# A convolution stage laid out anew: weight lows on GpSimd, pairs of channel groups summed as one, more native fp32 products

## The chip, the core and the metric

The kernel runs on one core of a Trainium2 chip. Its engines are TensorE (PE, with its weight loads as PEld), VectorE (DVE), ScalarE (ACT), GpSimd (POOL) and SyncE (SP), which issues the DMA transfers. Each engine works through its own list of instructions in order; an instruction starts when the semaphores that it waits on are there. The metric is the device time of one execution in microseconds.

## The reference

One inference step of a two-layer decoder trunk over 256 prompt tokens and 8 sample tokens, which share the weights. Layer 0 has a Conformer convolution as its mixer, layer 1 an mLSTM; each is followed by a layer norm, a gated feed-forward block with a three-tap convolution, another norm, and a gated per-layer embedding. The change lies in the mixer of layer 0:

```python
def conformer_conv(x, past, w_in, b_in, w_dw, b_dw, ln_g, ln_b, w_out, b_out):
    a, gt = jnp.split(x @ w_in + b_in, 2, axis=-1)      # 2048 -> 2 x 2048
    u = a * jax.nn.sigmoid(gt)
    y, new_past = causal_dwconv(u, past, w_dw, b_dw)    # 31 taps per channel
    y = jax.nn.silu(layer_norm(y, ln_g, ln_b))
    return y @ w_out + b_out, new_past
...
x = layer_norm(ALPHA * x + mix, ln_mix_g[i], ln_mix_b[i])
```

## The kernel before

Everything is kept feature by feature: a tile holds 128 channels (one group) by 264 tokens, and 2048 channels are 16 groups. A matrix product runs over 16 pieces of 128 input channels (k). Weights come from memory in fp32, three raw buffers of four k pieces by 512 columns. Most are split into a high part `whi` (a cast on ACT to fp32r) and a low part `wlo` (raw minus high, on DVE or POOL), and a product is three fp32r matmuls: high weight with the high and the low part of X (`XH`, `XL`), low weight with `XH`. A native product takes the raw weight and fp32 `X` in one instruction, which the trace shows as two records, and needs neither high nor low part.

The mixer goes through the 16 channel groups in blocks (`BLOCKS`), seven of two groups and two of one. `conv_mixer` calls `wblock` for a block's gate and value columns (L216 the load, L226 native products, L234 the cast, L235 the low, L250 to L259 the matmuls). `NAT` says which pairs of k pieces are native, `PLO` which lows POOL makes; DVE makes the others. Then the block's gates: a sigmoid on ACT (L546), which frees the gate's accumulator, the product `U` = value times gate in PSUM on DVE (L141), and its copy to SBUF (`us4`, L555).

The 31 taps of a group are shared out. Two go to ACT alone (L557, L559). `GT` taps are a product on ACT (L564) and a sum on POOL (L138, `cscr`). `PT` taps, in the last blocks, are matmuls with a diagonal weight matrix (L588); POOL makes the diagonals in the first block (L504). The others are one scalar-tensor-tensor on DVE each, from `U` into `Y` (L141). A join on DVE (L138, `Y<-Y,cscr`) adds POOL's sums to `Y`. The sample tokens need the past state times the taps (`xs`, `SCM`).

Behind the last block comes the layer norm: `ln_pre` sums the first 12 groups, shifts them by their mean and sums their squares, `ln` adds the last four groups and normalises. Then the output projection starts, in which `WOL` names the lows of the first block that POOL makes. `residual` scales X by ALPHA for the sum behind it.

A scheduler sets each engine's order ahead of time by priorities (`tc.high_priority`): casts and lows may be made up to five steps ahead of their matmuls (five `hlp` buffers). DMA issues all stand in SP's list.

Of the kernel before, what the change touches and what calls it, by code (L numbers as in the profile page):

```python
# [108 lines left out]
def _body(ctx, tc, nc, I, O):  # L109
# [94 lines left out]
    def wblock(W, cols, rhs, nk, acc, k0=0, loe=None, hook=None, fine=False, native=None, hold=(), lag=0, stage=0, side=None):  # L204
# [3 lines left out]
        for kg in range(0, nk, 4):  # L208
            kn = min(4, nk - kg)
            raw = rawp.tile([P, 4, 512], F32, name="raw")  # L210
            for ka, step in ([(0, 2), (2, 2)] if fine else [(0, kn)]):
# [8 lines left out]
            for h0 in range(0, kn, 2):  # L220
                for f in (side or {}).get(kg + h0, ()):
                    f()
                if native and native(kg + h0):
                    for kc in (kg + h0, kg + h0 + 1):
# [6 lines left out]
                r = raw[:, h0:h0 + 2, :width]  # L231
# [12 lines left out]
                for k2 in range(2):  # L244
# [32 lines left out]
    def ln_pre(Y, pm=None):  # L277
        a = t4("lna")
        tt(a, Y[:, 0:4], Y[:, 4:8], ALU.add)
        tt(a, a, Y[:, 8:12], ALU.add)  # L280
# [198 lines left out]
    def conv_mixer():  # L479
# [15 lines left out]
        def diags():  # L495
# [20 lines left out]
        late = []  # L516
        for bi, (c0, n) in enumerate(blocks):
            last = bi == len(blocks) - 1
            acc = accs(2 * n)
            wblock(W, [(D + c0 * P, n * P), (c0 * P, n * P)], x_rhs, NC, acc,  # L520
                   loe=lambda k, bi=bi: g if _pick(PLO[bi], k // 2) else v,
                   native=lambda k, bi=bi: _pick(NAT[bi], k // 2) or (bi == 0 and k // 2 in N0), hook=load if bi == 0 else None, fine=bi == 0)
            if bi == DGB:
                diags()
            if last:
# [5 lines left out]
                emb = embed(embed_load(0, pl), None, [us4[:, 4:8], us4[:, 0:4]])  # L531
                with tc.high_priority(PREP):
                    shift, sd, sq = ln_pre(Y, accs(1)[0])
            for q in SCM.get(bi, ()):
# [4 lines left out]
                tt(xs, xs, w.unsqueeze(2).to_broadcast([P, 4, NB, 30]), ALU.mult)  # L539
                ys = Y[:, 4 * q:4 * q + 4, SEQ:]  # L540
                v.tensor_reduce(ys, xs, AX.X, ALU.add)
                tt(ys, ys, pc("cv_b_dw", 4 * q, 4).unsqueeze(2).to_broadcast([P, 4, NB]), ALU.add)
# [4 lines left out]
            Z = []
            gt = GT[bi]
            for j in range(n):
                ch, a = c0 + j, acc[n + j]  # L550
# [8 lines left out]
                act(z[:, 1:SEQ], w[:, 0:SEQ - 1], AF.Copy, scale=pc("cv_w_dw", ch * CW + 29))  # L559
                Z.append(z)  # L560
            for t in range(28, 28 - gt, -1):
                for j in range(n):
                    z2 = slot(4, 8)
                    act(z2[:, 30 - t:SEQ], us4[:, (2 * bi + j) % 8, 0:226 + t], AF.Copy, scale=pc("cv_w_dw", (c0 + j) * CW + t))  # L564
                    tt(Z[j][:, 30 - t:SEQ], Z[j][:, 30 - t:SEQ], z2[:, 30 - t:SEQ], ALU.add, e=g)
            if (c0 + n) % 4 == 0:

                q = c0 + n - 4
                w = pc("cv_w_dw", q * CW, 4 * CW).rearrange("p (c t) -> p c t", t=CW)[:, :, 30:31]
                uw = smp.tile([P, 4, NB], F32, name="uw")  # L570
                tt(uw, us[:, q:q + 4], w.to_broadcast([P, 4, NB]), ALU.mult)
                tt(Y[:, q:q + 4, SEQ:], Y[:, q:q + 4, SEQ:], uw, ALU.add)
            pt = PT.get(bi, 0)
# [5 lines left out]
            def join(n=n, c0=c0, Z=Z):  # L579
# [525 lines left out]
```

## Time and profile before

| | us |
|---|---|
| median of 3 runs | 2574.08 (2572.9 to 2576.8) |
| the profiled execution | 2575.43 |
| its span | 2573.7 |
| PE busy | 2514.4 (98%) |
| DVE busy | 1656.2 (64%) |
| ACT busy | 1284.8 (50%) |
| POOL busy | 318.2 (12%) |

The shares are means over stages that differ: POOL has nearly all its work in the first tenth of the span, which is the convolution stage. Times in the rows below count from the start of the span.

### The profile page before, as it was taken

To read this page: it belongs to the slowest core of one execution; us is meant where nothing else is said; L and a number is where in the kernel's file an instruction comes from. 1 tells how busy PE (TensorE), PEld (TensorE's weight loads), DVE (VectorE), ACT (ScalarE), POOL (GpSimd) and SP (SyncE) were. 2 spreads that over 40 slices of the span, in tenths; PEclk is the share of its full clock that TensorE was granted. 3 is DMA by queue.
4 is the path that set the end of the run, shared out by engine and by line. 5 is a ranking of instruction groups with operands and counts; after the bars stand their busy time and mean duration, and the time that the engine had idled before them with its cause. 6 is when DMAs were issued, how large, how long until landed. Compare 5 with 4: busy or idle time off the path is not lost.

```text
span 2573.7 us, 47727 instructions
## 1 busy us (share of the span) xinstructions
PE 2514.4 (98%) x20130; PEld 2489.2 (97%) x20130; DVE 1656.2 (64%) x2382; ACT 1284.8 (50%) x1801; POOL 318.2 (12%) x320
## 2 busy tenths in 40 slices
PE   8898999999999999999999999999999999999999
PEld 8897999999999999999999998999999999999999
DVE  6999786555444555478667777685555445555595
ACT  5676555444334444356557665464444334444363
POOL 7898120000000000011000000020000000000020
PEclk9999999999999999999999999999999999999999
DMA  7546445655555556555677777555565556556553
GB/s 248 178 133 195 159 159 183 195 180 181 180 181 181 180 167 222 179 171 181 211 236 237 248 257 238 198 173 181 169 192 182 181 174 187 180 179 205 176 173 133
DMA packets 266696, 486.56 MB, mean 189 GB/s; under 512 B 12362, under 2 KB 68426, under 8 KB 265938
## 3 DMA queue, kind: packets, MB, share of 16 engines
q1 hardware_dynamic: 266482, 483.52, 58.2%
q8 instruction: 157, 2.57, 0.4%
q14 instruction: 57, 0.47, 0.1%
HBM read 465.77 MB, written 19.68 MB: 189 GB/s over the span
## 4 chain that ended last, share of the span: by engine, by line
PE 86%; DVE 5%; DMA 3%; POOL 3%; issue 2%; ACT 1%; SPq 0%; POOLq 0%; DVEq 0%; ACTq 0%
PE acc L253 27%; PE acc L250 27%; PE acc L252 24%; PE acc L259 3%; POOL cscr L138 1%; DMA out_cT<-X 1%; DVE wlo L235 1%; POOL wlo L235 1%; DVE Y L138 1%; PE acc L452 1%; DVE Y L141 1%; DMA X<-in_cT 1%; DMA spare<-scr 1%; PE acc L226 1%; POOL u L504 0%
## 5 line engine op out<-in xcount | busy, mean ns | idle before, releaser
L235 DVE TENSOR_TENSOR wlo<-raw,whi 128x1024 fp32r<-128x1024 f32 (+1 forms) x770 | 960.0, 1252 | 801.7 <-ACT whi L234 751.0
L234 ACT CAST whi<-raw 128x1024 fp32r<-128x1024 f32 x812 | 846.0, 1045 | 999.7 <-PE acc L252 952.6
L253 PE MATMUL acc<-XH,wlo 128*128 128x264 f32 x4264 | 1190.7, 286 | 17.4 <-DVE wlo L235 9.3
L250 PE MATMUL acc<-XH,whi 128*128 128x264 f32 x4264 | 1193.0, 286 | 6.6 <-ACT cscr L546 5.0
L252 PE MATMUL acc<-XL,whi 128*128 128x264 f32 x3696 | 1049.0, 285 | 0.0
L253 PEld LDWEIGHTS acc<-XH,wlo 128*128 128x128 f32 x4264 | 803.1, 189 | 20.5 <-DVE wlo L235 10.3
L250 PEld LDWEIGHTS acc<-XH,whi 128*128 128x128 f32 x4264 | 801.0, 189 | 9.9 <-ACT cscr L546 5.4
L252 PEld LDWEIGHTS acc<-XL,whi 128*128 128x128 f32 x3696 | 700.8, 190 | 0.2
L235 POOL TENSOR_TENSOR wlo<-raw,whi 128x1024 fp32r<-128x1024 f32 (+1 forms) x42 | 97.6, 2327 | 1696.1 <-DVE X L138 1506.0
L253 PE MATMUL acc<-ha,wlo 128*128 128x264 f32 x1024 | 290.0, 285 | 0.0
L250 PE MATMUL acc<-ha,whi 128*128 128x264 f32 x1024 | 288.4, 285 | 0.0
L252 PE MATMUL acc<-ha,whi 128*128 128x264 f32 x960 | 271.9, 284 | 0.0
L250 PE MATMUL acc<-xo,whi 128*128 128x264 f32 x768 | 221.4, 289 | 2.2 <-ACT vv L877 1.5
L253 PE MATMUL acc<-xo,wlo 128*128 128x264 f32 x768 | 218.9, 287 | 0.0
L252 PE MATMUL acc<-xo,whi 128*128 128x264 f32 x720 | 207.7, 289 | 0.0
L253 PEld LDWEIGHTS acc<-ha,wlo 128*128 128x128 f32 x1024 | 193.1, 189 | 0.0
L250 PEld LDWEIGHTS acc<-ha,whi 128*128 128x128 f32 x1024 | 191.9, 188 | 0.1
L252 PEld LDWEIGHTS acc<-ha,whi 128*128 128x128 f32 x960 | 181.3, 189 | 0.1
L250 PEld LDWEIGHTS acc<-xo,whi 128*128 128x128 f32 x768 | 144.6, 188 | 3.3 <-ACT vv L877 1.7
L253 PEld LDWEIGHTS acc<-xo,wlo 128*128 128x128 f32 x768 | 144.7, 189 | 0.6
L252 PEld LDWEIGHTS acc<-xo,whi 128*128 128x128 f32 x720 | 135.9, 189 | 0.6
L138 POOL TENSOR_TENSOR cscr<-cscr 128x254 f32<-128x254 f32 (+10 forms) x140 | 123.8, 909 | 11.6 <-ACT cscr L564 10.4
(283 smaller groups left out, 2495.4 us busy)
## 6 DMA issues: line engine op xcount, KB each, us to landing
raw<-in_ff_w_gate SPq DMA_DIRECT2D x88, 1024.0 KB, 5.1
raw<-in_ff_w_up SPq DMA_DIRECT2D x88, 1024.0 KB, 5.1
raw<-in_ff_w_down SPq DMA_DIRECT2D x88, 1024.0 KB, 5.0
raw<-in_pl_w_gate SPq DMA_DIRECT2D x32, 1024.0 KB, 5.1
raw<-in_ml_w_in SPq DMA_DIRECT2D x32, 1024.0 KB, 5.9
raw<-in_cv_w_in SPq DMA_DIRECT2D x48, 512.0 KB, 4.8
raw<-in_cv_w_out SPq DMA_DIRECT2D x16, 1024.0 KB, 5.1
raw<-in_ml_w_in SPq DMA_DIRECT2D x32, 512.0 KB, 5.1
```

The lines of the kernel that those rows point to most:

```text
L138: return e.tensor_tensor(o, a, b, op)
L141: return v.scalar_tensor_tensor(o, a, sc, b, op0, op1)
L226: pe.matmul(acc[j], raw[:, kc - kg, j * P:(j + 1) * P], X[:, kc], start=kc == 0, stop=kc == nk - 1)
L234: whi = s.copy(hi[:, :, :width], r)
L235: wlo = e.tensor_tensor(lo[:, :, :width], r, f32(hi[:, :, :width]), ALU.subtract)
L250: pe.matmul(acc[j], wh, xh, start=kc == 0, stop=False)
L252: pe.matmul(acc[j], wh, xl, start=False, stop=False)
L253: wlast[0] = pe.matmul(acc[j], wl, xh, start=False, stop=not lag and kc == nk - 1)
L259: pe.matmul(acc[j], whs[j], xl, start=False, stop=lag > 0 and k0_ == nk - 1)
L452: po(pe.matmul(acc, w[:, k, j * P:(j + 1) * P], pt[:, k], start=k == 0, stop=k == 1))
```

## The change

Only the mixer of layer 0 changes. There are ten blocks now: two of one group, six of two, two of one. In a block of one group (256 columns) a raw buffer, a high and a low tile hold twice as many k pieces, so a cast or a low is 1024 elements wide there too, and `NAT` picks among four groups of four pieces; the first and the last block are native throughout. Of 512 products 192 are native (56 before). All lows of the input projection go to POOL. A tap sum of a block of two groups is one POOL instruction of 2 by 254 elements (one each before), and `GT` is 5 or 6 in most blocks. The joins move to POOL and come one block later (the last two stay on DVE), as do the state products and the sums for the sample tokens. ACT makes the diagonals, 30 instead of 37. The gates have a higher priority (`GLU`). The norm's shift and squares for groups 0 to 7 are made in the block of groups 10 and 11 (`ln_first`), those of groups 8 to 11 in the block of group 14 (`ln_second`). `residual` waits for the norm's last ACT operation. One transfer stores the last 30 tokens of four groups instead of one.

```diff
-BLOCKS = [(0, 2), (2, 2), (4, 2), (6, 2), (8, 2), (10, 2), (12, 2), (14, 1), (15, 1)]
-GT = [8, 7, 12, 6, 13, 8, 7, 11, 7]
-PT = {6: 4, 7: 9, 8: 20}
-NAT = [0, 1, 0, 0, 0, 0, 0, 3, 7]
-PLO = [0, 6, 8, 2, 3, 5, 5, 7, 4]
-SCM = {1: (0, 1), 2: (2, 3)}
+BLOCKS = [(0, 1), (1, 1), (2, 2), (4, 2), (6, 2), (8, 2), (10, 2), (12, 2), (14, 1), (15, 1)]
+GT = [6, 6, 5, 5, 5, 5, 5, 9, 8, 6]
+PT = {7: 2, 8: 8, 9: 18}
+NAT = [4, 1, 2, 2, 2, 2, 2, 3, 2, 4]
+PREPS = (6, 8)
+SCM = {1: (0,), 2: (1,), 3: (2,), 4: (3,)}
...
-        for kg in range(0, nk, 4):
-            kn = min(4, nk - kg)
+        kq = 4 if width == 256 else 2
+        for kg in range(0, nk, 2 * kq):
+            kn = min(2 * kq, nk - kg)
             raw = rawp.tile([P, 4, 512], F32, name="raw")
...
+            if width == 256:
+                raw = raw.rearrange("p a (b m) -> p (a b) m", b=2)
...
-                g.tensor_scalar(d, ident, pc("cv_w_dw", c * CW + t), 0.0, ALU.mult, ALU.add)
+                act(d, ident, AF.Copy, scale=pc("cv_w_dw", c * CW + t))
...
-                   loe=lambda k, bi=bi: g if _pick(PLO[bi], k // 2) else v,
-                   native=lambda k, bi=bi: _pick(NAT[bi], k // 2) or (bi == 0 and k // 2 in N0), hook=load if bi == 0 else None, fine=bi == 0)
+            wblock(W, [(D + c0 * P, n * P), (c0 * P, n * P)], x_rhs, NC, acc, loe=lambda k: g,
+                   native=lambda k, bi=bi, kq=6 - 2 * n: _pick(NAT[bi], k // kq, NC // kq), hook=load if bi == 0 else None, fine=bi == 0)
...
-                with tc.high_priority(PREP):
-                    shift, sd, sq = ln_pre(Y, accs(1)[0])
...
-                tt(xs, xs, w.unsqueeze(2).to_broadcast([P, 4, NB, 30]), ALU.mult)
+                tt(xs, xs, w.unsqueeze(2).to_broadcast([P, 4, NB, 30]), ALU.mult, e=g)
...
+            with tc.high_priority(GLU):
+                for j in range(n):
+                    act(sg[:, j], acc[j], AF.Sigmoid, bias=pc("cv_b_in", NC + c0 + j))
+                if last:
+                    act(dummy, sq[:, 0:1], AF.Sqrt)
...
             for t in range(28, 28 - gt, -1):
+                z2 = slot(4, n)
                 for j in range(n):
-                    z2 = slot(4, 8)
...
-                    tt(Z[j][:, 30 - t:SEQ], Z[j][:, 30 - t:SEQ], z2[:, 30 - t:SEQ], ALU.add, e=g)
...
+                tt(Z[:, :, 30 - t:SEQ], Z[:, :, 30 - t:SEQ], z2[:, :, 30 - t:SEQ], ALU.add, e=g)
+
+            def join(e, n=n, c0=c0, Z=Z):
+                o = Y[:, c0:c0 + n, 1:SEQ]
+                tt(o, o, Z[:, :, 1:SEQ], ALU.add, e=e)
...
+            while joins:
+                joins.pop(0)(g if bi < nb - 1 else v)
+            joins.append(join)
...
+            if bi == PREPS[0]:
+                sum2 = smp.tile([P, 2, T], F32, name="sum2", tag="sf")
+                shift, sd = ln_first(Y, sum2, accs(1)[0])
+            if bi == PREPS[1]:
+                sq = ln_second(Y, shift, sd, sum2)
...
-        residual("cv_b_out", 0)
+        residual("cv_b_out", 0, ac.last)
```

The lists below show three places. The first is the start of ACT's list (`XH<-X` are the casts of X, `whi` those of the weights, `u_110<-ident,par` the diagonals). Before:

```order
L198 ACT_TABLE_LOAD
L198 CAST XH<-X 128x264 x4
L234 CAST whi<-raw 128x1024
L198 CAST XH<-X 128x264 x2
L234 CAST whi<-raw 128x1024
```

And of the changed kernel:

```order
L197 ACT_TABLE_LOAD
L197 CAST XH<-X 128x264 x10
L546 ACTIVATE u_110<-ident,par 128x128 x16
L197 CAST XH<-X 128x264 x6
L238 CAST whi<-raw 128x1024 x2
L589 ACT_TABLE_LOAD
L589 ACTIVATE cscr<-acc_112,par 128x264
```

The weight casts now stand behind all casts of X and 16 diagonals; the first sigmoid (L589) follows two of them.

The second is POOL's list in the middle of the stage (`wlo` are lows, `cscr<-cscr` tap sums). Before, in the block of groups 4 and 5:

```order
L235 TENSOR_TENSOR wlo<-raw,whi 128x1024
L138 TENSOR_TENSOR cscr<-cscr 128x247
L138 TENSOR_TENSOR cscr<-cscr 128x248
L138 TENSOR_TENSOR cscr<-cscr 128x246
L138 TENSOR_TENSOR cscr<-cscr 128x247
L138 TENSOR_TENSOR cscr<-cscr 128x245
L138 TENSOR_TENSOR cscr<-cscr 128x246
L138 TENSOR_TENSOR cscr<-cscr 128x244
```

In the changed kernel, from the sums of groups 6 and 7 to the join of the same groups:

```order
L137 TENSOR_TENSOR cscr<-cscr 128x2x254
L137 TENSOR_TENSOR cscr<-cscr 128x2x253
L239 TENSOR_TENSOR wlo<-raw,whi 128x1024
L137 TENSOR_TENSOR cscr<-cscr 128x2x252
L239 TENSOR_TENSOR wlo<-raw,whi 128x1024 x2
L137 TENSOR_TENSOR cscr<-cscr 128x2x251
L239 TENSOR_TENSOR wlo<-raw,whi 128x1024
L137 TENSOR_TENSOR cscr<-cscr 128x2x250
L239 TENSOR_TENSOR wlo<-raw,whi 128x1024 x2
L137 TENSOR_TENSOR Y<-Y,cscr 128x2x255
```

Five sums of both groups stand among six lows, and the join that DVE made is the last row.

The third is DVE's list around the gate of the last group (`acc_2744` before and `acc_2295` now are its `U`). Before:

```order
L138 TENSOR_TENSOR Y<-Y,cscr 128x255 x2
L141 SCALAR_TENSOR_TENSOR acc_2744<-acc_2655,par,cscr 128x256
L141 SCALAR_TENSOR_TENSOR us<-acc_2655,par,cscr 128x8
L141 SCALAR_TENSOR_TENSOR sd<-lnshift,sd 128x264
L138 TENSOR_TENSOR Y<-Y,lnshift 128x1056 x3
L138 TENSOR_TENSOR uw<-us,par 128x32
L235 TENSOR_TENSOR wlo<-raw,whi 128x1024
L138 TENSOR_TENSOR Y<-acc_2771,Y 128x247
```

In the changed kernel:

```order
L140 SCALAR_TENSOR_TENSOR Y<-U,par,Y 128x228
L140 SCALAR_TENSOR_TENSOR acc_2295<-acc_2250,par,cscr 128x256
L140 SCALAR_TENSOR_TENSOR us<-acc_2250,par,cscr 128x8
L140 SCALAR_TENSOR_TENSOR Y<-U,par,Y 128x227
L137 TENSOR_TENSOR Y<-acc_2327,Y 128x245
L140 SCALAR_TENSOR_TENSOR Y<-U,par,Y 128x226
L137 TENSOR_TENSOR Y<-acc_2331,Y 128x245
L137 TENSOR_TENSOR Y<-Y,cscr 128x255
```

The three subtractions of the shift from 1056 elements and the work on `sd` no longer follow the last gate; taps and the added accumulators do.

## Rows read from the trace of the kernel before

**Rows 1.** Windows, two stretches: length, busy by engine (instructions), PE clock, DMA, GB/s.

```profile
0.00:266.50 266.50, 233.41 (x1600) 221.08 (x1600) 238.33 (x434) 172.81 (x324) 225.37 (x226) 0.95 0.57 186
266.50:2574.00 2307.50, 2281.03 (x18530) 2268.07 (x18530) 1417.92 (x1949) 1111.95 (x1478) 92.86 (x94) 1.00 0.59 189
```

**Rows 2.** Windows, middle of the stage (PE, PEld, DVE, ACT, POOL).

```profile
30.00:231.00 201.00, 181.02 (x1308) 174.00 (x1307) 190.38 (x367) 132.93 (x255) 189.32 (x176) 0.95 0.51 161
```

**Rows 3.** Waits of PE to 266.5 us: total, times, longest.

```profile
PE acc L253 <- POOL wlo L235: 8.0, 7, 3.3
PE acc L351 <- DVE sq L138: 7.0, 1, 7.0
PE acc L253 <- DVE wlo L235: 6.5, 3, 2.8
...
PE acc L250 <- ACT cscr L546: 5.0, 2, 3.7
```

**Rows 4.** Groups by line on DVE to 266.5 us: busy, mean ns, idle before.

```profile
L235 DVE TENSOR_TENSOR wlo<-raw,whi 128x1024 fp32r<-128x1024 f32 (+1 forms) x31 | 51.9, 1675 | 10.8 <-ACT whi L234 10.6
L138 DVE TENSOR_TENSOR Y<-Y,cscr 128x255 f32<-128x255 f32 x16 | 17.2, 1083 | 0.3 <-POOL cscr L138 0.2
...
L138 DVE TENSOR_TENSOR xs<-xs,par 128x960 f32<-128x960 f32 x4 | 9.4, 2352 | 1.3 <-DMA xs<-in_sconv 1.3
```

**Rows 5.** Groups by line on POOL to 266.5 us: the diagonals.

```profile
L504 POOL TENSOR_SCALAR u<-ident,par 128x128 f32<-128x128 f32 x16 | 11.4, 733 | 12.8 <-DMA par<-in_par 12.8
L504 POOL TENSOR_SCALAR dg<-ident,par 128x128 f32<-128x128 f32 x21 | 8.4, 421 | 0.0
```

**Rows 6.** Windows, one of split products and two of native products.

```profile
20.00:25.00 5.00, 5.00 (x43) 5.00 (x42) 3.82 (x7) 2.73 (x4) 5.00 (x8) 1.00 1.08 382
220.00:225.00 5.00, 5.00 (x25) 4.25 (x24) 5.00 (x11) 5.00 (x14) 4.92 (x6) 1.00 0.85 264
225.00:230.00 5.00, 5.00 (x24) 4.29 (x23) 5.00 (x14) 3.68 (x9) 4.76 (x7) 1.00 0.91 299
```

**Rows 7.** Timeline of POOL and DVE, around 60 and 165 us: start, length.

```profile
59.43 1.40 POOL L138 TENSOR_TENSOR cscr<-cscr 128x252 f32<-128x252 f32 x2
60.79 4.76 POOL L235 TENSOR_TENSOR wlo<-raw,whi 128x1024 fp32r<-128x1024 f32 x2
59.76 6.00 DVE L141 SCALAR_TENSOR_TENSOR Y<-U,par,Y 128x239 f32<-128x239 f32 x16
164.69 2.40 POOL L138 TENSOR_TENSOR cscr<-cscr 128x249 f32<-128x249 f32 x2
165.24 1.26 DVE L235 TENSOR_TENSOR wlo<-raw,whi 128x1024 fp32r<-128x1024 f32 x1
```

**Rows 8.** Groups on PE to 232 us: one of a split product's three matmuls.

```profile
L250 PE MATMUL acc<-XH,whi 128*128 128x264 f32 x456 | 131.9, 293 | 5.4 <-ACT cscr L546 5.0 <-ACT whi L234 0.5
```

**Rows 9.** Timeline of PE and DVE, start and end of the stage.

```profile
4.99 5.22 PE L226 MATMUL acc<-X,raw 128*128 128x264 f32 x16 [4.99 <-DMA raw<-in_cv_w_in]
216.27 14.22 PE L226 MATMUL acc<-X,raw 128*128 128x264 f32 x56
237.78 6.28 DVE L138 TENSOR_TENSOR Y<-Y,lnshift 128x1056 f32<-128x1056 f32 x3
239.26 8.58 PE L588 MATMUL acc<-u,dg 128*128 128x235 f32 x42
256.69 0.41 DVE L138 TENSOR_TENSOR Y<-acc,Y 128x247 f32<-128x247 f32 x1
266.53 0.39 PE L250 MATMUL acc<-XH,whi 128*128 128x264 f32 x1 [0.23 <-ACT XH L368]
```

**Rows 10.** Timeline of ACT and POOL near the start.

```profile
14.95 0.92 ACT L399 ACTIVATE X<-X,par 128x264 f32<-128x264 f32 x2 [0.43 <-DMA par<-in_par]
34.22 1.68 ACT L564 ACTIVATE cscr<-u,par 128x254 f32<-128x254 f32 x4
34.68 0.79 POOL L138 TENSOR_TENSOR sf<-sf,par 128x352 f32<-128x352 f32 x1
```

More of the change, by code (lines that the diff above doesn't have):

```diff
@@ L219, in wblock @@
                     at += w
-            for h0 in range(0, kn, 2):
+            for h0 in range(0, kn, kq):
                 for f in (side or {}).get(kg + h0, ()):
@@ L223, in wblock @@
                 if native and native(kg + h0):
-                    for kc in (kg + h0, kg + h0 + 1):
+                    for kc in range(kg + h0, kg + h0 + kq):
                         for j in range(nm):
@@ L243, in wblock @@
                     continue
-                for k2 in range(2):
+                for k2 in range(kq):
                     kc = kg + h0 + k2
@@ L273, in bc4, with ln_sum @@
         return ap.unsqueeze(1).to_broadcast([P, n, T])
-    def ln_pre(Y, pm=None):
+    def ln_sum(Y, n):
         a = t4("lna")
         tt(a, Y[:, 0:4], Y[:, 4:8], ALU.add)
-        tt(a, a, Y[:, 8:12], ALU.add)
+        for q in range(2, n):
+            tt(a, a, Y[:, 4 * q:4 * q + 4], ALU.add)
         tt(a[:, 0:2], a[:, 0:2], a[:, 2:4], ALU.add)
@@ L301, in ln_pre, with ln_first, ln_second @@
         return c, sd, sq
+    def ln_first(Y, sum2, pm):
+        sd = ln_sum(Y, 2)
+        c = ln_shift(Y, sd, 2, pm)
+        b = t4("lnb")
+        act(b, Y[:, 0:4], AF.Square)
+        b2 = t4("lnb2")
+        act(b2, Y[:, 4:8], AF.Square)
+        tt(b, b, b2, ALU.add)
+        tt(sum2[:, 0], b[:, 0], b[:, 1], ALU.add)
+        tt(sum2[:, 1], b[:, 2], b[:, 3], ALU.add)
+        return c, sd
+    def ln_second(Y, c, sd, sum2):
+        y = Y[:, 8:12]
+        tt(y, y, bc4(c), ALU.subtract)
+        b = t4("lnb")
+        act(b, y, AF.Square)
+        a = t4("lna")
+        tt(a[:, 0:2], Y[:, 8:10], Y[:, 10:12], ALU.add)
+        tt(b[:, 0:2], b[:, 0:2], b[:, 2:4], ALU.add)
+        tt(a[:, 0], a[:, 0], a[:, 1], ALU.add)
+        tt(sd, sd, a[:, 0], ALU.add)
+        tt(b[:, 0:2], b[:, 0:2], sum2, ALU.add)
+        sq = t1("sq")
+        tt(sq, b[:, 0], b[:, 1], ALU.add)
+        return sq
     def ln(Y, gn, bn, off, outs, silu=False, acc=None, emb=(), pq=None):
@@ L488, in slot @@
             ring[0] += 1
-            return scr[:, first + ring[0] % n]
+            k = first + 2 * (ring[0] % 4)
+            return scr[:, k:k + n]
         us4, dg = hB(F32, "u4")
@@ L566, in conv_mixer @@
+            joins.append(join)
             if (c0 + n) % 4 == 0:
                 q = c0 + n - 4
[L569 to L573, printed above, removed]
+                uw = smp.tile([P, 4, NB], F32, name="uw", bufs=2)
+                for c in range(4):
+                    act(uw[:, c], us[:, q + c], AF.Identity, bias=pc("cv_b_dw", q + c), scale=pc("cv_w_dw", (q + c) * CW + 30))
+                tt(Y[:, q:q + 4, SEQ:], Y[:, q:q + 4, SEQ:], uw, ALU.add, e=g)
@@ L591, in join_pe @@
                     tt(o, acc[:, 30 - t0:SEQ], o, ALU.add)
-            late.append(join_pe)
-            if bi == len(blocks) - 2:
-                late.insert(len(late) - 1, join)
-            elif not last:
-                join()
-            if last or not pt:
+            if pt:
+                late.append(join_pe)
+            if last:
                 for f in late:
                     f()
-                late = []
-            if last:
-                join()
+                while joins:
+                    joins.pop(0)(v)
                 for mm, out in emb[:EC]:
```

85 lines of the change are left out of this document (43 added, 42 removed).

## The prediction

> **What bounds the kernel now.** I read the busy time in two stretches first. From 266.5 us on, PE is busy 2281 of 2307 us [rows 1], and of the change only the scaling of X reaches into it, so only the convolution stage is open: it ends at 266.53, when the first matmul of the output projection starts [rows 9]. In the 201 us between 30 and 231 us VectorE is busy 190 us, GpSimd 189 and TensorE 181 [rows 2]: no engine has room, and PE is not the fullest. PE's waits say what ends last: the low halves of the weights from POOL (8.0 us) and DVE (6.5), the sigmoids that free accumulators (5.0), and 7.0 us for the sum of squares at the end [rows 3]. A wait costs more than its length, since the granted clock drops behind it: the 266.5 us have a mean clock of 0.95, the rest 1.00 [rows 1].
>
> What should PE have needed? At full clock 43 fp32r matmuls fit in 5.00 us, 0.116 us each, so a product of a 128 by 128 weight piece with X in three matmuls costs 0.349 us. In the native stretches 24.5 records fit in 5 us, two records a product: 0.408 us [rows 6]. The input projection has 16 times 32 = 512 products, 456 of them split [rows 8] and 56 native: 159.1 + 22.9 = 182 us. It took from 5.0 to 230.5 us [rows 9], 225.5 us: **43.5 us are waits, slow clock and the start**. Then 36.0 us pass to the first output matmul.
>
> Why are DVE and POOL so full? A DVE low takes 1.675 us on average [rows 4], one of 1024 elements 1.26 where it got through at once [rows 7]; a join of 255 elements takes 1.083 on average [rows 4], an addition of 247 took 0.41 beside an idle POOL [rows 9]. On POOL a sum takes 0.70 us while DVE runs only taps (16 taps in 6.00 us, their source in PSUM), but two sums took 2.40 us when a DVE low started among them [rows 7]. Taps leave POOL alone; two-input DVE operations between SBUF tiles and POOL's operations wait for each other.
>
> **The change, engine by engine.** *DVE* loses its lows in the projection (31 in the stage, 51.9 us; three of the output projection stay, some 4 us), all joins but two (17.2, keeps 0.8), the four state products (9.4) [rows 4]: 73 us. It gains 340 - 287 = 53 taps at 6.00/16 = 0.375 us [rows 7]: 20 us. A pair block then costs it 48 taps, 18.0 us, and about 2.5 us of gates and one reduction, 20.5 us.
>
> *POOL* gets every low of the projection: 40 instead of 28 wide and 4 half ones. With 2.38 us a low (4.76 for two) and 0.70 a sum of 254 [rows 7], a line through both gives 1.25 us for a pair's 508 elements; two singles, 1.40, are the upper bound. It loses the 37 diagonals (19.8 us [rows 5]). A pair block costs 6 lows (14.3), 5 pair sums (6.3), a join (1.25): 21.8 us; where a state product is added, 2.2 us more (the 352-element product took 0.79 [rows 10], times 960/352), 24.0. Its work from its first low to its last in the block of group 14: 40 lows 95, sums of the first seven blocks 12 x 0.70 + 25 x 1.25 = 40, joins 6, state products 9: 150 us.
>
> *ACT* takes the 30 diagonals and gives up 46 of 140 tap products, each 1.68/4 = 0.42 us [rows 10]. A pair block costs it 6 casts, 10 products and two gates, some 15 us: hidden.
>
> *PE* pays: 192 products are native instead of 56. 320 x 0.349 + 192 x 0.408 = 111.7 + 78.3 = 190.0 us, 8 us more. The page FP8 and Floating Point Precision of the Trainium skill (TensorE Precision Notes) has true fp32 as four passes. By that rule a native product would be 4 x 0.116 = 0.465 us, the projection 201 us and the forecast 11 us later; the row has 0.408, and the row decides. A pair block is then 48 x 0.349 + 16 x 0.408 = 23.3 us on PE, against 21.8 to 24.0 on POOL and 20.5 on DVE. PE becomes the bound, with POOL close behind.
>
> *The start.* The first block (one group, all native) needs no low: 32 x 0.408 = 13.1 us from 5.0, done at 18. Then PE needs the first low. ACT has by then 16 diagonals that wait for the parameters, which landed at 14.95 [rows 10], ahead of six X casts (2.2 us) and the first weight cast (1.05), and POOL 2.38. If the parameters land at 12, with fewer bytes ahead of them, and a diagonal costs 0.3, this is at 22.4; with 14.95 and 0.42 (a tap product twice as wide) at 27. I take 24: 6 us of wait, in the sum.
>
> *The body.* 24 + (190.0 - 13.1) = 200.9 us, if POOL keeps pace. Laying the 21.8 to 24.0 us of each block beside PE's 23.3, POOL delivers each low 0 to 4 us ahead, so some are late, and the clock falls then. The norm's operations on DVE in the blocks of groups 8 to 13 (some 15 us) hold POOL up too. Below, this loss is 0; above, 25 us, most of what before loses. I take 8, a fifth of the 43.5, since DVE's two-input operations, which made most of the collisions, are gone from five of ten blocks: 209.
>
> *The tail.* Before, DVE after its last gate still had three subtractions of 6.28 us, joins and the squares' sums, and the last accumulator was added at 256.69 [rows 9], 9 us after PE had it. Now sums, shift and squares lie in earlier blocks. Behind the last native product PE has one statistics matmul (0.6), 12 diagonal products of the blocks before (42 records in 8.58 us [rows 9], 0.408 each: 4.9 us) and the last group's 18 (7.3): 12.8 us. The last gate must come before those 18: it is queued behind DVE's taps and may be 5 us late, just covered. DVE's other work there, about 6 us, fits beside. From the last added accumulator to the first output matmul before took 266.53 - 256.69 = 9.8 us, kept. A table load is new ahead of the square root, since the sigmoid of the last block now stands behind the early one; it runs beside the subtractions: 0 to 1.3 us, taken as 0. Tail 22.6 us. The scaling of X by ALPHA, 16 operations of 0.42 us on ACT, moves behind the norm; five weight casts made ahead and four among the activations cover 9 groups of 2.8 us; without that cover it costs up to 6.7.
>
> **Sum.** 209 + 22.6 = 231.6 us in place of 266.5: 34.9 us less. The profiled execution took 2575.43 us for a span of 2573.7; 2575.43 - 34.9 = 2540.5, and from the median 2574.08 it is 2539.2. I forecast **2540**.
>
> **Rivals.**
> - *POOL becomes the bound.* For: every low waits in one queue, behind sums that wait for ACT and joins that wait for DVE. Against: with taps alone beside it POOL keeps 2.38 and 0.70 [rows 7]. If its 150 us take a tenth more, 15 us are added to a start at 22 and the block ends move by 10 to 15: 2550 to 2556.
> - *The tail keeps its 36 us.* If DVE is late with the last block's taps and gate, the diagonal matmuls wait for the gate: 13.4 us more, 2553.
> - *Slower than before.* POOL and DVE go on colliding: the taps or the gates hold POOL's operations up as DVE's lows do, 1.2 us a single sum [rows 7]. Lows that wait for one DVE operation of 1.26 us take 3.6, pair sums 2.4: 40 x 3.6 + 25 x 2.4 + 12 x 1.2 + 15 = 233 us in place of 150; less the 8 already counted the stage ends 75 us later than forecast, 2615. It decides from POOL's 150 us becoming 193, 29% more (34.9 + 8 over 150). The pure tap stretch speaks against it.
> - *Native products cost more than 0.408 us.* If a native product took four matmuls' time, 0.465, PE's 192 would need 11 us more: 2551. The 49 records in two full-clock stretches [rows 6] speak against it. This is the four-pass rule of the Trainium skill cited above.
> - *Nothing comes of it.* PE's extra 8 us, the 6 us wait, and late lows eat what DVE gains: 2571 to 2577. That needs 35 us of new waits beside PE's 190; before has 43.5 with two engines full.
>
> **How the numbers follow.** About 0.2%, 5 us, is what a measurement of this kernel can tell. Chances: the forecast, within 2530 to 2550, 0.58; POOL as the bound 0.13; the long tail 0.10; better than 2530 (no loss in the body, 8 us, and an early start) 0.06; dear native products 0.03; nothing 0.04; slower 0.06. The range goes from 2528 to 2560; outside it lie the last two and the ends of the others, some 0.15. Faster 0.90, same 0.04, slower 0.06.
>
> **What would show it.** The first native block should end near 18 us, with one PE wait of some 6 us behind it for a POOL low; pair blocks should be 23 to 25 us apart (sigmoids), POOL lows at 2.4 and pair sums at 1.25 us, DVE idle between blocks; the last native product near 209, the first output matmul near 232, and no 7 us wait for the squares. Pair sums above 1.6 us, or PE waits for lows of over 15 us in sum, prove me wrong in the body; a gate of group 15 later than 6 us behind its product does in the tail.

## The result and the profile after

| | before | after |
|---|---|---|
| median of 4 runs, us | 2574.21 (2572.9 to 2576.8) | 2552.45 (2550.97 to 2552.83) |
| ratio | | 0.9916 [0.9901, 0.9931] |
| span of the profiled execution, us | 2573.7 | 2549.2 |
| last native product done, us | 230.5 | 216.9 |
| first matmul of the output projection, us | 266.53 | 244.02 |

The change made the kernel 21.8 us faster. The forecast was 34.9 us, 2540; the time lies in the range. The stage ends 22.5 us earlier, in place of 34.9: 13.6 us of it lie before the end of the last native product, 8.9 behind it. The other 2.0 us of the span's difference come later. native_alone (below) has the instructions of the kernel before there and needs 4.0 us less for them than that kernel's execution, so these 2.0 can't be put down to the change.

The first view is that of the windows: the stage, the rest, and the middle of the stage (length, then PE, PEld, DVE, ACT, POOL, clock, DMA share, GB/s).

```profile
0.00:244.00 244.00, 231.86 (x1450) 214.14 (x1450) 188.29 (x433) 143.88 (x290) 188.66 (x133) 0.99 0.63 203
244.00:2549.00 2305.00, 2279.96 (x18530) 2268.19 (x18530) 1418.36 (x1949) 1118.15 (x1494) 92.37 (x94) 1.00 0.58 190
...
30.00:231.00 201.00, 196.63 (x1301) 184.22 (x1301) 169.83 (x393) 116.84 (x230) 176.44 (x116) 0.99 0.59 190
```

Between 30 and 231 us PE is now busy 196.6 us, 181.0 before [rows 2], DVE 169.8 (190.4) and POOL 176.4 (189.3), and the clock is 0.99 (0.95). PE has become the fullest, as forecast. The view of PE's waits up to the first output matmul, with total, times and longest, is short:

```profile
PE acc L228 <- DMA raw<-in_cv_w_in: 4.0, 1, 4.0
PE acc L257 <- POOL wlo L239: 3.4, 2, 1.9
PE lnm L392 <- ACT cscr L589: 2.9, 1, 2.9
PE acc L254 <- ACT whi L238: 1.5, 1, 1.5
```

The 14.5 us of waits for lows, the 5.0 for sigmoids and the 7.0 for the sum of squares [rows 3] have become 3.4 and 1.5 us for lows and a cast, 2.9 for a statistics matmul, and nothing for the squares. POOL's groups by line (busy, mean ns, idle before):

```profile
L239 POOL TENSOR_TENSOR wlo<-raw,whi 128x1024 fp32r<-128x1024 f32 x42 | 102.1, 2445 | 24.5 <-ACT whi L238 24.5
L137 POOL TENSOR_TENSOR cscr<-cscr 128x508 f32<-128x508 f32 (+16 forms) x60 | 64.7, 1079 | 12.9 <-ACT cscr L608 10.7
L137 POOL TENSOR_TENSOR Y<-Y,cscr 128x510 f32<-128x510 f32 (+1 forms) x8 | 10.2, 1270 | 0.2
L137 POOL TENSOR_TENSOR xs<-xs,par 128x960 f32<-128x960 f32 x4 | 8.4, 2092 | 0.1
```

A low costs 2.445 us (forecast 2.38), a pair join 1.27 (1.25), and the first pair sum below shows 1.29 (1.25): POOL's prices were read rightly. Two of the 42 lows belong to the output projection.

Three places of the timeline carry the rest. First, PE and ACT at the start:

```profile
4.03 17.15 PE L228 MATMUL acc<-X,raw 128*128 128x264 f32 x64 [4.03 <-DMA raw<-in_cv_w_in]
...
22.71 0.50 PE L254 MATMUL acc<-XH,whi 128*128 128x264 f32 x2 [1.52 <-ACT whi L238]
25.14 0.51 PE L257 MATMUL acc<-XH,wlo 128*128 128x264 f32 x2 [1.93 <-POOL wlo L239]
...
13.13 4.78 ACT L546 ACTIVATE u<-ident,par 128x128 f32<-128x128 f32 x16 [1.56 <-DMA par<-in_par]
...
21.61 1.99 ACT L238 CAST whi<-raw 128x1024 fp32r<-128x1024 f32 x2 [1.83 <-DMA raw<-in_cv_w_in]
```

Second, native stretches of PE in the pair blocks (a third one, at 72.21, lies between the first two), and a join with the first pair sum on POOL:

```profile
60.19 3.72 PE L228 MATMUL acc<-X,raw 128*128 128x264 f32 x16
...
84.98 3.72 PE L228 MATMUL acc<-X,raw 128*128 128x264 f32 x16
...
97.00 3.72 PE L228 MATMUL acc<-X,raw 128*128 128x264 f32 x16
...
176.68 1.29 POOL L137 TENSOR_TENSOR Y<-Y,cscr 128x510 f32<-128x510 f32 x1
...
177.93 1.29 POOL L137 TENSOR_TENSOR cscr<-cscr 128x508 f32<-128x508 f32 x1
```

Third, PE, ACT and DVE in the tail:

```profile
202.71 14.18 PE L228 MATMUL acc<-X,raw 128*128 128x264 f32 x63
...
215.47 3.87 ACT L238 CAST whi<-raw 128x1024 fp32r<-128x1024 f32 x4
218.04 1.25 DVE L239 TENSOR_TENSOR wlo<-raw,whi 128x1024 fp32r<-128x1024 f32 x1
...
219.25 0.47 ACT L589 ACTIVATE cscr<-acc,par 128x264 f32<-128x264 f32 x1
...
219.81 0.68 PE L392 MATMUL lnm<-sd,onesD 128*128 128x264 f32 x2 [2.92 <-ACT cscr L589]
...
220.32 8.44 PE L640 MATMUL acc<-u,u 128*128 128x245 f32 x32
220.43 2.16 DVE L239 TENSOR_TENSOR wlo<-raw,whi 128x1024 fp32r<-128x1024 f32 x1
...
223.37 0.48 DVE L140 SCALAR_TENSOR_TENSOR acc<-acc,par,cscr 128x256 f32<-128x256 f32 x1
...
228.60 5.78 PE L640 MATMUL acc<-u,dg 128*128 128x244 f32 x28
...
234.41 0.42 DVE L137 TENSOR_TENSOR Y<-acc,Y 128x248 f32<-128x248 f32 x1 [1.50 <-PE acc L640]
...
244.02 0.39 PE L254 MATMUL acc<-XH,whi 128*128 128x264 f32 x1 [0.30 <-ACT XH L409]
```

**What a product costs.** A native stretch of 16 records lasts 3.72 us; the first record lasts 0.39, so they start every 3.33 / 15 = 0.222 us, and a product, two records, costs 0.444 us. From the native stretch at 60.19 to that at 97.00 PE does three such stretches (48 x 0.222 = 10.66 us) and, between them, 70, 74 and 70 fp32r matmuls: (36.81 - 10.66) / 214 = 0.122 us each, so a split product costs 0.367. The forecast had 0.408 and 0.349: it divided 5.00 us by the instructions that a window lists [rows 6], but a window lists every instruction that reaches into it, so the count is too high by one or two.

The last native product ended near 216.9 (forecast 209), the tail took 27.1 us (22.6).

### The profile page after: what moved, and what is told of

Its sections match the earlier page's. It is cut to its first block, busy times and chain, and to the rows that moved or that the text cites. A ratio compares the mean times of both kernels' runs of the same rounds, so it can differ in the third digit from the quotient of the medians.

```text
span 2549.2 us, 47224 instructions
## 1 busy us (share of the span) xinstructions
PE 2511.8 (99%) x19980; PEld 2482.3 (97%) x19980; DVE 1606.6 (63%) x2381; ACT 1262.0 (50%) x1783; POOL 281.0 (11%) x227
## 4 chain that ended last, share of the span: by engine, by line
PE 89%; DVE 4%; DMA 4%; ACT 2%; POOL 1%; issue 1%; SPq 0%; DVEq 0%; POOLq 0%; ACTq 0%
PE acc L254 28%; PE acc L257 28%; PE acc L256 25%; PE acc L263 3%; DVE Y L140 1%; PE acc L228 1%; PE acc L493 1%; DMA raw<-in_cv_w_in 1%; DMA spare<-scr 1%; DMA out_cT<-X 1%; DMA X<-in_cT 1%; PE acc L640 1%; DVE wlo L239 1%; ACT whi L238 0%; POOL cscr L137 0%
## 5 line engine op out<-in xcount | busy, mean ns | idle before, releaser
L239 DVE TENSOR_TENSOR wlo<-raw,whi 128x1024 fp32r<-128x1024 f32 x742 | 913.4, 1236 | 789.9 <-ACT whi L238 741.6
L238 ACT CAST whi<-raw 128x1024 fp32r<-128x1024 f32 x792 | 827.0, 1048 | 1014.5 <-PE acc L256 955.1
L254 PE MATMUL acc<-XH,whi 128*128 128x264 f32 x4128 | 1150.6, 286 | 2.9 <-ACT whi L238 1.5
L257 PE MATMUL acc<-XH,wlo 128*128 128x264 f32 x4128 | 1142.2, 285 | 5.0 <-POOL wlo L239 3.4
L256 PE MATMUL acc<-XL,whi 128*128 128x264 f32 x3560 | 1007.7, 284 | 0.0
L257 PEld LDWEIGHTS acc<-XH,wlo 128*128 128x128 f32 x4128 | 772.5, 189 | 6.2 <-POOL wlo L239 3.8
L254 PEld LDWEIGHTS acc<-XH,whi 128*128 128x128 f32 x4128 | 773.0, 189 | 5.5 <-ACT whi L238 2.1
L256 PEld LDWEIGHTS acc<-XL,whi 128*128 128x128 f32 x3560 | 673.5, 189 | 0.4
L239 POOL TENSOR_TENSOR wlo<-raw,whi 128x1024 fp32r<-128x1024 f32 x50 | 121.7, 2444 | 1718.7 <-DVE X L137 1506.0
L140 DVE SCALAR_TENSOR_TENSOR Y<-U,par,Y 128x242 f32<-128x242 f32 (+12 forms) x335 | 131.2, 454 | 11.5 <-ACT u L597 6.8
```

Of the source, the lines that this page charges most:

```text
L140: return v.scalar_tensor_tensor(o, a, sc, b, op0, op1)
L238: whi = s.copy(hi[:, :, :width], r)
L239: wlo = e.tensor_tensor(lo[:, :, :width], r, f32(hi[:, :, :width]), ALU.subtract)
L254: pe.matmul(acc[j], wh, xh, start=kc == 0, stop=False)
L256: pe.matmul(acc[j], wh, xl, start=False, stop=False)
L257: wlast[0] = pe.matmul(acc[j], wl, xh, start=False, stop=not lag and kc == nk - 1)
```

## The experiments

All twelve start from the changed kernel, but for the last, which starts from the one before. Of single executions the first output matmul tells more than the time: behind it the fourteen profiled executions needed 2302.0 to 2307.2 us, though their instructions there hardly differ. The end of the last native product divides the stage into its body and its tail.

| kernel | last native product done, us | first output matmul, us | against 244.02 | median, us | ratio to before |
|---|---|---|---|---|---|
| before | 230.5 | 266.53 | +22.5 | 2574.21 | 1 |
| changed | 216.9 | 244.02 | | 2552.45 | 0.9916 [0.9901, 0.9931] |
| fewer_native | 229.9 | 255.65 | +11.6 | 2560.43 | 0.9946 [0.9932, 0.9959] |
| more_native | 217.5 | 248.06 | +4.0 | 2554.28 | 0.9925 [0.9913, 0.9938] |
| lows_shared | 226.8 | 255.59 | +11.6 | 2561.54 | 0.9953 [0.994, 0.9965] |
| norm_late | 214.9 | 247.92 | +3.9 | 2554.15 | 0.9927 [0.9915, 0.994] |
| fewer_late78 | 211.0 | 241.61 | -2.4 | 2547.39 | 0.9898 [0.9885, 0.9912] |
| stat_behind | 217.1 | 243.70 | -0.3 | 2547.59 | 0.9903 [0.989, 0.9917] |
| joins_dve | 217.0 | 248.00 | +4.0 | 2552.38 | 0.9915 [0.9901, 0.9929] |
| single_sums | 217.8 | 246.21 | +2.2 | 2556.30 | 0.9927 [0.9914, 0.9939] |
| gate_first | 217.7 | 243.99 | 0.0 | 2551.50 | 0.9916 [0.9903, 0.993] |
| best | 211.2 | 244.25 | +0.2 | 2549.35 | 0.9907 [0.9892, 0.9922] |
| two_input_dve | 225.8 | 257.47 | +13.5 | 2566.03 | 0.9973 [0.9963, 0.9983] |
| native_alone | 228.0 | 257.75 | +13.7 | 2562.67 | 0.9958 [0.9945, 0.997] |

**The price of a product, and which engine is the bound.**

```diff
-NAT = [4, 1, 2, 2, 2, 2, 2, 3, 2, 4]
+NAT = [4, 1, 1, 1, 1, 1, 1, 2, 2, 4]     fewer_native
+NAT = [4, 1, 3, 3, 3, 3, 3, 4, 2, 4]     more_native
```

> One native step less in each of the six pair blocks behind the first two: 48 products go from native to split, and GpSimd gets 6 more lows of 2.45 us. Theory (PE is the bound of the body; a native product costs 0.444 us and a split one 0.367): PE's work falls by 48 x 0.077 = 3.7 us, GpSimd's rises by 14.7 us from 170 to 185 of the 196 us between 21 and 217, still under PE's 187; the first output matmul comes at 240 to 242 in place of 244.0, and the time is 2549 to 2551. Rival (GpSimd with its one queue is the bound, PE only looks busy): the stage ends 8 to 14 us later, PE waits for lows grow from 3 to over 10 us, time 2560 to 2567.

> One native step more in each of the same six blocks: 48 products go from split to native, 6 lows fewer on GpSimd. Theory (PE the bound, 0.077 us a product): 3.7 us more on PE, time 2556, waits for lows at zero but for the start. Rival (GpSimd the bound): 14.7 us less on GpSimd, the stage ends 4 to 10 us earlier, time 2543 to 2549.

fewer_native came out at the rival's time, but not by the rival's mechanism. The native stretch of the block of group 1 and the last one of the block of groups 10 and 11, with 40 products changed between them, in fewer_native, the changed kernel and more_native:

```profile
35.20 3.73 PE L228 MATMUL acc<-X,raw 128*128 128x264 f32 x16
155.92 3.72 PE L228 MATMUL acc<-X,raw 128*128 128x264 f32 x16
```
```profile
35.31 3.73 PE L228 MATMUL acc<-X,raw 128*128 128x264 f32 x16
159.03 3.72 PE L228 MATMUL acc<-X,raw 128*128 128x264 f32 x16
```
```profile
33.85 3.73 PE L228 MATMUL acc<-X,raw 128*128 128x264 f32 x16
160.26 3.72 PE L228 MATMUL acc<-X,raw 128*128 128x264 f32 x16
```

From one to the other are 120.72, 123.72 and 126.41 us: 3.00 us less and 2.69 more, 0.075 and 0.067 us a product, where the spacing gives 0.077. By the prices above the five blocks between need 123.6 us in the changed kernel. So PE is the bound of these blocks on both sides, and POOL makes its additional lows in time. What cost fewer_native its gain is one wait of PE, in its waits to 300 us:

```profile
PE acc L293 <- DVE sd L137: 15.0, 1, 15.0
```

L293 is the matmul for the norm's shift. The scheduler had placed it ahead of the block of groups 12 and 13; DVE's sum for it was done 15 us later. In more_native the stage ends 4.0 us later, near the theory's 3.7, but that is luck: its last native product ends only 0.6 us later, since its start is 1.5 us earlier and the wait of 1.5 us for a low at 176.8 us is gone. The other 3.4 us lie in the tail, where the statistics matmul waits 5.1 us in place of 2.9. fewer_late78 keeps the fewer native products and makes the norm's first sums, shift and its matmul one block later:

```diff
-PREPS = (6, 8)
+PREPS = (7, 8)
```

> As fewer_native (48 products from native to split, 6 more lows on GpSimd), but the sums and the shift of groups 0 to 7 are made one block later, so that the matmul for the shift stands behind 56 products of the block of group 14 in PE's list and not ahead of those of groups 12 and 13. Theory (a native product is 0.077 us dearer than a split one, and the 15 us that PE waited in fewer_native were only for that one matmul's place): the wait is gone, PE's last native product ends 3 to 4 us ahead of that of the changed kernel (213 for 216.9), and the time is 2547 to 2551, if the norm's work, now closer to the end, doesn't make the last gates late. Rival (GpSimd can't make six more lows): pair blocks 26 us apart or more, waits for lows over 8 us, time 2557 to 2563.

The matmul runs at 177.67 us there, in the block of groups 12 and 13, behind some 50 of its 64 products (not in that of group 14, as expected). DVE's sum for it was done at 173.8, in fewer_native at 174.5. The wait is gone and the last native product ends near 210.9, 6 us earlier than in the changed kernel; the place of one matmul decided between 2560 and 2547. Of the 6 us 2.4 reach the output projection: the statistics matmul waits 5.0 us, and the last sigmoid runs at 220.87 only.

**What was gained in the body.** One part undone, then two, then one part alone.

```diff
-    loe=lambda k: g,
+    loe=lambda k: v if k // 2 in (1, 4, 5) else g,          lows_shared, two_input_dve
-    joins.pop(0)(g if bi < nb - 1 else v)
+    joins.pop(0)(v)                                         joins_dve, two_input_dve
-    tt(xs, xs, w.unsqueeze(2)..., ALU.mult, e=g)
+    tt(xs, xs, w.unsqueeze(2)..., ALU.mult)                 joins_dve, two_input_dve
...
-    NAT = [0, 1, 0, 0, 0, 0, 0, 3, 7]
+    NAT = [1, 2, 2, 2, 2, 2, 2, 4, 8]                       native_alone, in the kernel before
```

> The split of the lows is undone in part: 18 of the 42 lows of the input projection go back to VectorE, all else as in the changed kernel. Theory (what the change gained in the body is that VectorE has no two-input work between SBUF tiles beside GpSimd): VectorE gets 18 lows of 1.26 to 1.68 us, 23 to 30 us, and stands at 182 to 189 of 196 us; lows and sums of GpSimd that meet them lengthen, gates come late behind taps, and the stage ends 8 to 15 us later, 2560 to 2568, with PE waits for lows or sigmoids over 8 us. Rival (who makes the lows is worth nothing, since PE is the bound and both engines have room: VectorE 159, GpSimd 170 of 196): within 3 us of 2552.

> Joins and the four products for the sample tokens go back from GpSimd to VectorE: 8 joins and 4 products, 18.5 us less on GpSimd (170 to 152 of 196 us), some 18 us more on VectorE (159 to 177). Theory (in the changed kernel PE is the bound, but two-input work on VectorE beside GpSimd costs more than its own time, as in lows_shared, which lost 9 us for 18 lows): 2 to 6 us slower, 2554 to 2559, by late gates or lows. Rival (both engines have room for it): within 1.5 us of 2552.

> lows_shared and joins_dve together: 18 lows, the joins and the four products are VectorE's again, with blocks, native products, pair sums, diagonals and the norm in parts as in the changed kernel. Theory (what the change gains in the body comes from taking two-input work between SBUF tiles off VectorE): lows_shared moved the first output matmul by 11.6 us, joins_dve by 4.0; together VectorE is nearly full (173 + 12 to 18 of 196 us) and the costs add or more than add: first output matmul at 259 to 268, time 2565 to 2574. Rival (the two cost the same slack once): at 256 to 258, time 2561 to 2564.

> The kernel before with one part of the change alone: two native steps in the pair blocks behind the first and more in the single ones, 160 native products in place of 56, so 12 wide lows fewer on VectorE and GpSimd; all else as before. Theory (PE lost some 33 us of the projection's 225 to engines that were full, and native products buy room on them at 0.077 us each): 104 x 0.077 = 8 us more on PE, 12 lows of 1.7 to 2.4 us less on the others, 25 us in sum; the stage ends 2 to 8 us earlier, time 2566 to 2572. Rival (the room isn't used, since gates and joins on VectorE hold the chain): 5 to 8 us slower, 2579 to 2582.

In the traces lows_shared moved 19 of the projection's 40 lows (the expectation counts 18 of 42). It lost 11.6 us of the stage (theory 8 to 15), 9.9 of them in the body. joins_dve lost 4.0 us (its median shows none of it), all in the tail, where the statistics matmul waits 5.5 us for DVE's taps. Both together lost 13.5. That is nearly the sum of 15.6, though the first output matmul at 257.5 lies in the rival's band of 256 to 258 and only the time, 2566.0, in the theory's; VectorE had a little room left to share. The window from 21 to 217 us of two_input_dve:

```profile
21.00:217.00 196.00, 186.76 (x1244) 176.54 (x1245) 184.39 (x376) 108.47 (x214) 112.99 (x68) 0.97 0.56 180
```

DVE is busy 184 of 196 us and POOL only 113, and PE waits for gates, in its waits from 30 to 300 us:

```profile
PE acc L640 <- ACT u L597: 4.1, 1, 4.1
PE acc L254 <- DVE us L140: 3.7, 1, 3.7
...
PE acc L254 <- ACT cscr L589: 1.9, 1, 1.9
```

None of the three is in the changed kernel. I put the loss down to a full VectorE more than to the collisions, but no run separates the two, and the collisions are there: POOL's sums take 1.315 us on average against 1.079 above. In the changed kernel POOL's lows keep their 2.445 us beside 335 taps on DVE. The page SBUF — State Buffer of the Trainium skill (Who interferes with whom) says that a DVE instruction with at most one SBUF input, outside its two-port modes, does not contend with GpSimd, and that one with two contends with a GpSimd instruction that reads SBUF; the lows beside the taps, one of whose two tensors lies in PSUM, agree.

native_alone surprised me: more native products, alone in the kernel before, end the stage 8.8 us earlier and save 10.5 us, more than the theory's 2 to 8. Its 104 products more cost PE 8 us, and its last native stretch still ends at 227.96, that of before at 216.27 + 14.22 = 230.49 [rows 9]:

```profile
215.34 12.62 PE L226 MATMUL acc<-X,raw 128*128 128x264 f32 x56
```

So 2.5 us were gained in the body and 6.2 in the tail, where the wait of 7.0 us for the sum of squares is gone without the norm in parts. Between 30 and 231 us DVE and POOL were busy 177 and 162 us there instead of 190 and 189. POOL made 11 lows fewer, DVE one; yet DVE's 16 joins took 0.727 us each instead of 1.083 [rows 4] and its state products 1.42 instead of 2.35, so a part of the room came from fewer collisions. The joins' line there:

```profile
L138 DVE TENSOR_TENSOR Y<-Y,cscr 128x255 f32<-128x255 f32 x16 | 11.5, 727 | 4.1 <-POOL cscr L138 4.1
```

So, in this order of taking the parts: native products 8.8 us (266.5 to 257.8; body 2.5, tail 6.2); the other parts without the move to POOL 0.3 (to 257.5, that is two_input_dve, which has 192 native products, not 160; by the medians they cost 3.4); lows, joins and products to POOL 13.5 (to 244.0; body 8.9, tail 4.6). Another order could divide it otherwise.

**Two smaller parts.**

```diff
-    tt(Z[:, :, 30 - t:SEQ], Z[:, :, 30 - t:SEQ], z2[:, :, 30 - t:SEQ], ALU.add, e=g)
+    for j in range(n):                                               single_sums
+        tt(Z[:, j, 30 - t:SEQ], Z[:, j, 30 - t:SEQ], z2[:, j, 30 - t:SEQ], ALU.add, e=g)
...
-    if last: act(dummy, sq[:, 0:1], AF.Sqrt)                         norm_late
-    if bi == PREPS[0]: ... ln_first(...)
-    if bi == PREPS[1]: ... ln_second(...)
+    if last: ... ln_first(...); ln_second(...)
```

> The tap sums of a pair block are made one group at a time again: 60 instead of 30 or so instructions, at 0.74 us a single against 1.29 a pair: 5 us more on GpSimd (170 to 175 of 196 us). Theory (PE is the bound and GpSimd keeps room): within 1.5 us of 2552. Rival (GpSimd is at its limit, so every microsecond counts): 4 to 6 us slower, 2556 to 2558.

> The norm in parts is undone: sums, shift and squares of groups 0 to 11 are all made in the last block, as before the change; all else is as in the changed kernel. Theory (the norm's work behind the last gates was what made the tail of before 36 us long): some 13 us of VectorE's work move behind the last native product, PE waits some 7 us for the sum of squares, the tail grows from 27 to 34 to 38 us, time 2559 to 2563. Rival (VectorE's idle time at the end covers it): within 3 us of 2552.

single_sums lies 2.2 us later in the trace, in an execution of 2551.64 us; its median, 2556.30, lies in the rival's band, but its five runs go from 2550.8 to 2557.6, so what a pair sum is worth stays open. norm_late, at 3.9 us later and a median 1.7 us higher, is nearer to its rival by the median and to neither in the trace. There PE waits 7.0 us, as forecast, though for `sd`, which DVE makes just behind the sum of squares; the tail is 5.9 us longer. But the last native product ends 2 us earlier, near 214.9: in these two traces the norm's early work costs the body a part of what it saves in the tail.

**The tail.**

```diff
+    wlast[0] = pe.matmul(acc[:, 30 - t:SEQ], diag[c0 + j, t], ...)   stat_behind, gate_first, best
+    po.last = wlast[0]            (the norm's first statistics matmul stands behind it)
...
+    hold=[(0, (last sigmoid, last gate))]   in the output projection's first block: gate_first, best
```

> The first statistics matmul of the norm, which waits 2.9 us for a PSUM buffer ahead of the diagonals, is put behind the last diagonal in PE's list; nothing else moves. Theory (PE is held there, and the diagonals behind it start late): 12 diagonals run from 217 to 222.3, PE then waits some 2 us for the copy of the last group's product (224.2), and the last 18 end near 232.4 in place of 234.2; with the statistics matmul then in the way for 0.4 us the first output matmul comes at 242.2 to 243.2, time 2550.5 to 2551.5, less than a median can tell, so the trace decides. Rival (VectorE's and GpSimd's own last work, taps to 231.9 and sums to 232.6, sets the end): first output matmul at 244 as now.

> As stat_behind, and the output projection's first casts and lows stand behind the last group's sigmoid (ScalarE) and gate (VectorE). In the changed kernel the sigmoid runs at 219.25, behind four casts of 3.87 us, and the gate at 223.37, behind two lows of 1.25 and 2.16 us; in stat_behind PE then waited 2.5 us for the gate's copy, and its clock was at 1.2 GHz for 3.41 us behind that wait. Theory (the tail is PE's chain of 30 diagonals, held up by the gate alone): sigmoid near 217.2, gate at 220 to 222, PE waits under 1 us and keeps its clock, the diagonals need 12.2 us in place of 13.9 and end at 229 to 231.5, first output matmul 239 to 241.5 against 243.7 in stat_behind. Rival (the work that was moved behind the gate, casts and lows, or the last taps and sums, is late next): first output matmul at 243 to 246, or new waits for lows behind it of over 2 us.

> fewer_late78 and gate_first together. In fewer_late78 the last native product ends at 210.9 (6 us ahead of the changed kernel), but the last sigmoid runs at 220.9 only, behind casts, and the first output matmul comes at 241.6. Theory (the gain of the body was lost in the tail by the order of ScalarE's and VectorE's lists): sigmoid near 211.5, gate at 213 to 217, first output matmul 234 to 238, time 2540 to 2544. Rival (VectorE, with the norm's parts so late, is the bound of the end: its taps of group 14 and the gate behind them can't come sooner): first output matmul 239 to 242, time 2545 to 2548.

In stat_behind the diagonals start 3.4 us earlier, at 216.91, but PE then waits 2.50 us for the last group's copy, and the granted clock falls behind that wait. Windows of the changed kernel, then of stat_behind:

```profile
217.00:220.00 3.00, 0.20 (x1) 1.00 0.00 0
220.00:224.00 4.00, 4.00 (x13) 0.63 0.30 75
```
```profile
220.00:224.00 4.00, 2.00 (x10) 1.00 0.25 51
224.00:228.00 4.00, 3.50 (x9) 0.57 1.04 393
```

The wait moved, the slow clock with it, and 0.3 us are left. Its median of 2547.6 is not explained by that: behind the first output matmul its execution needed 2302.0 us, the least of all. gate_first takes the wait down to 1.5 us, keeps the clock at 1.00, and the last diagonal is done 2 us earlier than in stat_behind; still the output projection starts at 243.99, by its rival, and PE waits 2.0 us for DVE's norm on the way. The sigmoid runs at 217.29, where it was expected, but the gate only at 223.15, 0.2 us earlier than in the changed kernel: without the lows, 31 taps and a join stand ahead of it. Its DVE:

```profile
210.06 12.04 DVE L140 SCALAR_TENSOR_TENSOR Y<-U,par,Y 128x234 f32<-128x234 f32 x31
222.21 1.02 DVE L137 TENSOR_TENSOR Y<-Y,cscr 128x255 f32<-128x255 f32 x1
223.15 0.48 DVE L140 SCALAR_TENSOR_TENSOR acc<-acc,par,cscr 128x256 f32<-128x256 f32 x1
...
223.68 2.85 DVE L239 TENSOR_TENSOR wlo<-raw,whi 128x1024 fp32r<-128x1024 f32 x1
...
227.09 1.74 DVE L239 TENSOR_TENSOR wlo<-raw,whi 128x1024 fp32r<-128x1024 f32 x1
...
229.07 1.49 DVE L239 TENSOR_TENSOR wlo<-raw,whi 128x1024 fp32r<-128x1024 f32 x1
...
235.70 0.42 DVE L137 TENSOR_TENSOR Y<-acc,Y 128x248 f32<-128x248 f32 x1
```

The lows, moved behind the gate, now stand ahead of DVE's last taps, and the last accumulator is added at 235.70 in place of 234.41. The kernel called best shows the same at 244.25: its sigmoid runs at 215.83, but the gate, behind 29 taps, at 219.71, PE waits 4.6 us for the gate's copy, and lows of 2.6, 2.4 and 1.7 us stand between DVE's last taps. So DVE's work, its taps as much as the order of its list, bounds the end of both. best is not the best of the kernels; fewer_late78 is. The ratio of fewer_late78 is 0.9898 where the changed kernel has 0.9916; the intervals overlap, the trace has it 2.4 us ahead at the first output matmul.

## Why the prediction was right, and where its steps were off

- **PE the bound, with POOL close behind:** right. PE waits 4.9 us in all for lows and a cast, the sigmoids of pair blocks (62.61, 87.41, 111.98, 136.32 and 161.70) lie 24.3 to 25.4 us apart (forecast 23 to 25), and 40 products more or fewer made five blocks longer or shorter by about what PE pays for them. The slower rival fell with it: POOL's prices rose by 3%, where the slower rival needed 29%.
- **The price of a product: the step that was mis-sized.** With 0.367 and 0.444 for 0.349 and 0.408 the projection costs PE 320 x 0.367 + 192 x 0.444 = 202.7 us, not 190.0: 12.7 us, about the whole miss of 12.4. The other terms nearly cancel: the tail is 4.5 us longer than forecast, the loss in the body 4.3 shorter. The additional native products cost 136 x 0.077 = 10.5 us, not 8. By the same prices the kernel before needed 456 x 0.367 + 56 x 0.444 = 192.2, so it lost 33.3 us of 225.5, not 43.5.
- **The rivals.** The time is outside 2530 to 2550, which I had held likeliest, and is that of three rivals: POOL as the bound (2550 to 2556), the long tail (2553), dear native products (2551). None of them is what happened alone. POOL kept pace; the tail of 27.1 us lies a third of the way from 22.6 to 36; a native product measured 0.444, between 0.408 and the rival's 0.465, and that rival left the split price as it was, which was too low as well.
- **Four passes.** By the rule of the Trainium skill's page FP8 and Floating Point Precision (TensorE Precision Notes) a native product would take 4 x 0.122 = 0.489 us, an estimate. The trace has 0.444, 3.6 fp32r matmuls: between the rule and the 0.408 that I set against it.
- **The start:** the first low was used at 25.14, forecast 24. The first block ended at 21.2, not 18: 64 records at 0.222 are 14.2 us, but it took 17.15, since its first 12 records start 0.44 us apart, twice the later distance (5, 6 and 7 records reach into the first three stretches of 2 us, 11 into each of the next five). The profile shows no wait between them, and a granted clock of 1.00, so the cause stays open. The kernel before shows it too: its first 16 records take 5.22 us [rows 9], 0.32 apart. The wait behind the block was 3.45 us in all, not 6.
- **The loss in the body:** 8 us forecast. The products behind the first block are 320 x 0.367 + 160 x 0.444 = 188.5 us; from 21.2 to 216.9 are 195.7, of which 3.45 are the start's waits: 3.7 us are left. About 1.5 of them are a slow clock behind those waits (0.63 and 0.52 in the windows from 26 to 30 us, where fp32r matmuls start 0.216 us apart), 1.5 the wait for a low at 176.8. Start, price and loss together are the 7.9 us between 209 and 216.9.
- **The tail:** 27.1 us for 22.6. The term that failed is "just covered": the gate of group 15 came at 223.37, 6.5 us behind its product, which by the prediction's own sign (later than 6 us) proves it wrong in the tail, and the statistics matmul, that I had at 0.6 us without a wait, held PE 2.92 us. The profile puts that wait down to the sigmoid; I take it that the matmul also needs the PSUM buffer that DVE's taps of groups 12 and 13 read until 219.7, and in more_native, fewer_late78, joins_dve and single_sums the profile puts its wait (4.2 to 5.5 us) down to those taps. Behind the wait the clock fell to 1.2 GHz for a while (0.63 in the window), and 30 diagonals took 13.9 us, not 12.2. The experiments show that taking the wait away alone gains 0.3 us, since gate, copy and DVE's last work are late next, and that moving lows out of the gate's way brings nothing, since DVE's taps are there.
- **Norm in parts:** assumed to remove the 7 us wait for squares; the wait is gone, and norm_late brings a wait of 7.0 us back. Its net worth is 3.9 us of the stage. But native_alone has no such wait either, with all of the norm in the last block, so it is not the only way to remove it.

What stays open: why executions differ by up to 5 us behind the first output matmul, and so how much of the medians' differences among kernels under 5 us apart is the change's.

## What to carry to other kernels

Where all engines are nearly full, buy room where it is cheap: here a native product cost PE 0.077 us and saved another engine an eighth of a low, 0.31 us. Take the price of a matmul from the distance of starts over a stretch without gaps, not from the instructions that a window lists. Look where a schedule written ahead of time puts the one matmul that waits for a slow engine, since PE does nothing behind it: its place was worth 13 us here, in an edit that was to move 4.

## What the runs showed of the hardware that was not expected

A native fp32 matmul of 128 by 128 with 264 columns cost 0.444 us, less than four fp32r matmuls (0.489) and more than the three of a split product (0.367). Each of the 20 waits of PE of 2.5 us or more between two matmuls of the stage, in the fourteen traces, was followed by a mean granted clock of 0.50 to 0.68 over the next 4 us (0.50 is 1.2 GHz throughout). After shorter ones it differed: 1.5 us in gate_first and 2.4 us in native_alone left it at 1.00, 1.9 us in two_input_dve (at 116.7 us) and 2.4 us in best were followed by 0.61.
